# A hybrid mLSTM and attention layer on one core: the turn of v, the norm's small operations and the sums of two products are placed and shared out differently

## The chip, the cores and the metric

The kernel runs on one core of a Trainium2 chip. The core has a matmul engine (PE, with a separate loader for its weights, PEld), and DVE, ACT and POOL for elementwise work; each works through its own queue in order. SP only issues transfers; POOL issues some too. The metric is the device time of one execution in microseconds (us), lower is better. The kernel before takes 1559.74 us, the median of three runs (1558.71 to 1560.47).

## The reference

One layer over 512 prompt frames and 64 frames of a running stream, with width 1024, in fp32:

```python
h = layer_norm(ALPHA * x + 0.5 * swiglu_ffn(x, ffn1_w_gu, ffn1_w_down), ln1_g, ln1_b)
mix, new_state = token_mixer(h, ...)
h = layer_norm(ALPHA * h + mix, ln2_g, ln2_b)
h = layer_norm(ALPHA * h + 0.5 * swiglu_ffn(h, ffn2_w_gu, ffn2_w_down), ln3_g, ln3_b)
```

The mixer multiplies h with one wide matrix, w_in, and splits the columns into the mLSTM's q, k, v, o, i, f, the attention's q, k, v, and two gates. The mLSTM has 4 heads of 256: a causal convolution of width 4 and a silu on q and k, then a chunked recurrence with exponential gates. The attention has 16 heads of 64 over a band of 8 chunks of 64 frames, with a bias by relative position; the running stream has 256 past keys and values. The two branches are projected, gated, added and multiplied with w_out. Besides the frames the new states are returned, the rows of k and v among them. layer_norm subtracts the mean, multiplies by rsqrt(variance + 1e-5), then by g, and adds b.

## The kernel before

All 576 frames stay in SBUF, features on the partitions: a tile (a "slot", tag s) is 128 features x 576 frames, worked on in two halves (hf) of columns. An fp32 factor is split into a high part (wh, hi), rounded to the matmul's input type, and a low part (wl, lo), the rest; a product is three matmuls: wh·hi, wh·lo, wl·hi. Large products are done in units of seven block products instead of eight (Strassen's way), for which sums of inputs are formed first: class Combos. Its method add makes four sums from two input tiles, make splits the sums in two parts.

**How a low part is made.** Either DVE subtracts the high part from the source, or add_lo (L195) does it: ACT copies the high part with a factor -1, and a transfer issued by POOL adds the source to it in flight. Weights pass through pump: SP loads a raw tile wr (two buffers), ACT makes wh, and DVE or add_lo makes wl (four buffers). Weights of w_in are named ("in", column); those in ADDED (L179) take add_lo, those in PIECES (L177) are converted in halves of 512 columns.

**What sets the order.** Python writes the program. The order on PE is written by hand: a model clock counts each matmul (122 for 288 columns), and later(dt, fn) places a piece dt units behind the present point. ACT, DVE, POOL and SP get their orders from a list scheduler; hot(n) and high_priority(offset=n) raise an operation in it, and tc.issue_after(x) forces an order. On the chip each queue is in order.

**The norm** (class Norm, L498 on; three times). stats (L633) sums on PE, takes the variance and rs = variance to the power -0.5 (on POOL), and builds dg, the identity scaled by rs, on DVE; centre (L699) subtracts the mean from the eight tiles of the half, the tiles in CP (L185 to L188) on POOL and the others on DVE; spread multiplies dg with ones on PE, so that each partition has every frame's rs, L_SPREAD or L_SPREAD1 (first FFN's norm) units behind stats; apply does the rest. The last half of the last norm is turned (L671): frames go to the partitions by transposes into four PSUM tiles of 512 columns, (block b, half of the features q). DVE subtracts the mean and multiplies by g from PSUM, then multiplies by rs and adds b, and SP stores: eight large DVE operations behind PE's last matmul.

**The first FFN** splits its sums with make (own parts all through add_lo). **The projection** (os_split, L1757 on) makes its sums with add, one turn of a loop for each of four pairs of tiles.

**The attention** runs over j, eight pairs of heads. att_qkv(j) (L1408) computes a pair's q, k, v; within it v_tr (L1442) transposes v so that frames lie on the partitions (tile vc; ACT evicts the high part, DVE the low), placed 8000 units behind its start for j of 2 and more, and v_past (L1431) splits the past values on POOL, at 9500. att_core(j) (L1515) follows: scores, the transposes of the probabilities, and the products with v. There ttr (L1541) adds the bias to a score tile and takes the row minimum (mx) in one DVE operation, at hot(20).

**The mLSTM head** h: the convolution (conv_rest, L1862) ends in a silu on ACT (qf, then qk), and weights (L2003), five blocks b placed 11000 + 2600 b units behind the head's start, multiplies q with k.

In the profile, L135 is the line of the helper that records every matmul, L145 that of transposes, L149 of ACT, L152, L155 and L159 of elementwise operations, L196 of add_lo's transfers; the tile's name tells which step it is.

Of the kernel before, what the change touches and what calls it, by code (L numbers as in the profile page):

```python
# [10 lines left out]
F32 = mybir.dt.float32  # L11
# [6 lines left out]
P = 128  # L18
# [70 lines left out]
def tile_layer(ctx: ExitStack, tc: tile.TileContext, ins, outs):  # L89
# [75 lines left out]
    def blank(out, like, behind=None):  # L165
# [10 lines left out]
    NH0, NH1 = 1, 6  # L176
    PIECES = {("in", 48), ("in", 40), ("in", 32)}  # L177

    ADDED = {("in", c + j) for c in (32, 40, 48) for j in range(2, KT)} | {("in", c) for c in (*range(2, 8), *range(10, 32), *range(56, 72))} \  # L179
        | {("gu2", 1, 1), ("gu2", 2, 0), ("gu2", 2, 1)}  # L180
# [4 lines left out]
    EARLY1 = [("in", 16), ("in", 17)]  # L185
    CP = (6, 7)
    GR = 2150
    L_MEAN, L_STATS, L_SPREAD, L_SPREAD1 = 300, 1440, 4920, 3600  # L188
    plan = []
# [308 lines left out]
    class Norm:  # L498
# [134 lines left out]
        def stats(self, hf):  # L633
            lp = self.lp
            s1, s2 = self.hs(self.s1, hf), self.hs(self.s2, hf)
            n = self.H[hf][1]
            nb = len(blocks_(n))
            st, bc = bank(), bank()[:, :n]
            self.sums(hf, st, 0, (s1,))
            mm(bc, ones_d, s1, True, True)  # L640
            self.sums(hf, st, 1, (s2,))
            with tc.high_priority(offset=HOT):
                rs, power = self.rsqrt(hf, st)

                dg = lp.tile([P, 320], F32, tag="sq", name=nm("dg"), bufs=2)[:, :n]
                tt(dg[:, 0:2 * P].rearrange("p (b c) -> p b c", c=P), ident.unsqueeze(1).to_broadcast([P, 2, P]),
                   rs[:, 0:2].unsqueeze(2).to_broadcast([P, 2, P]), ALU.mult)
                if nb == 3:
                    ts(dg[:, 2 * P:], ident[:, 3 * P - n:], rs[:, 2:3], None, ALU.mult)
            later(L_MEAN, lambda: self.centre(hf, bc, power))  # L650
            later(self.spread_at, lambda: self.spread(hf, dg))
# [16 lines left out]
        def turned(self, hf, dh, sq):  # L668
# [16 lines left out]
            with tc.high_priority(offset=HOT):  # L685
                m = self.lp.tile([P, 3], F32, tag="m2", name=nm("m"), bufs=2)
                act(m[:, :nb], st[:, 0:nb])
                rs, _ = self.rsqrt(hf, st)
            z = {}
            for q in range(2):  # L690
                for b in range(nb):
                    z[b, q] = slot(F32)[:, :512]
                    last = stt(z[b, q], pts[b, q], m[:, b:b + 1], self.gb[q], ALU.subtract, ALU.mult)
            with tc.issue_after(last.ins):
                for (b, q), t in z.items():
                    stt(t, t, rs[:, b:b + 1], self.gb[2 + q], ALU.mult, ALU.add)
                    SP.dma_start(outs["yt"][b, :, q * 512:(q + 1) * 512], t)

# [55 lines left out]
    class Combos:  # L754


        def __init__(self, xs, raw, sums, nx=NX):
            self.xs, self.raw, self.n, self.sums, self.nx = xs, raw, 0, sums, nx
            self.b = {}

# [3 lines left out]

        def add(self, i):
            r1, r2 = self.raw[4 + i], self.raw[i]
            a, b = slice(0, HT_), slice(HT_, T)
            u, v = self.sums[2 * i], self.sums[2 * i + 1]
            tt(u[:, a], r1[:, a], r1[:, b], ALU.subtract)
            stt(v[:, a], u[:, a], -1.0, r2[:, b], ALU.mult, ALU.subtract)  # L770
            tt(u[:, b], r2[:, b], r1[:, b], ALU.subtract)
            return stt(v[:, b], v[:, a], -1.0, r2[:, a], ALU.mult, ALU.subtract)

        @hot(80)
        def make(self, middle):
# [3 lines left out]
            for n, (ka, kb) in ((1, ("t2", "t4")), (0, ("t1", "t3"))):  # L779
                for i in range(4):  # L780

                    t, hi, lo = self.sums[2 * i + n], self.tile(), self.tile()
                    with tc.issue_after(after.ins) if after is not None else nullcontext():
                        last = ACT.activation(hi, t, AF.Copy)
                        self.added = add_lo(lo, hi, t)
                    d = self.b.setdefault(i, {})
                    d[ka], d[kb] = (hi[:, a], lo[:, a]), (hi[:, b], lo[:, b])
# [341 lines left out]
    def ffn(xs, n, gi, raw, final=None, prev=None):  # L1129
        hh = {}  # L1130
        with tc.tile_pool(name=nm("hr"), bufs=FT, side="right", reuse_waits="tile") as hr, \
# [20 lines left out]

            combos = Combos(xs, raw, [hr.tile([P, T], F32, tag="h", name=nm("h"), bufs=FT + 1) for _ in range(8)])
            j0 = CL[n]
            un = GateUp(n, j0, hr, None, None, combos)
# [251 lines left out]
    def att_qkv(j):  # L1407
# [30 lines left out]

        later(11500 if j < 2 else 9500, v_past)
        vf = vf0 if j == 0 else slot(F32)  # L1440
# [18 lines left out]
        elif j:  # L1459
            SP.dma_start(vf, AV[j])  # L1460
            SP.dma_start(outs["v"][:, j, :], vf)
        later((12500, 2240, 8000)[min(j, 2)], v_tr)

# [59 lines left out]
    def att_core(j, st):  # L1523
# [16 lines left out]

        @hot(20)  # L1541
        def ttr(out, ps, g, acc):
# [67 lines left out]
        def values_s(th, tl):  # L1610
# [6 lines left out]
            for e in range(2):  # L1617
                act(o_[64 * e:64 * e + 64, NP_:T], po[0:64, 64 * e:64 * e + 64])

        t = 4500 if j else 7000  # L1620
        for e in range(2):
# [115 lines left out]
    for j in range(6):  # L1737
# [3 lines left out]
        if j == 3:  # L1741
# [20 lines left out]
            def os_split():  # L1762
# [24 lines left out]
                for i in range(4):  # L1787
                    combos.sums[2 * i] = slot(F32)
                    combos.add(i)
                    halves(i, 1)  # L1790
# [73 lines left out]
    def conv_rest(R, ct, scale, room, tail=None):  # L1864
# [5 lines left out]
        hi, lo = room(), room()  # L1870
        with tc.issue_after(order["exp"].ins) if "exp" in order else nullcontext():
            for a, b, u in ((0, NP_, 0), (NP_, T, NP_ + 3)):
# [112 lines left out]
    def ml_early(h, st):  # L1985
# [34 lines left out]
        for b in range(5):  # L2020
            later(11000 + 2600 * b, lambda b=b: weights(b))

# [255 lines left out]
```

## Time and profile before

| | us |
|---|---|
| median of three runs | 1559.74 (1558.71 to 1560.47) |
| the profiled execution, as timed | 1559.26 |
| its span in the trace | 1557.5 |
| PE busy | 1533.1 |
| DVE busy | 1140.8 |
| ACT busy | 890.3 |
| POOL busy | 223.8 |

The profile is of one execution. The span runs from the first to the last recorded instruction; the 1.76 us beside it lie around the program. A row of a group of instructions gives line, engine, operation, output <- input with shape, then the count, the busy time and the mean of one; a number in square brackets is the engine's idle time just before an instruction, with what ended it.

### The profile page before, as it was taken

The numbers are of one execution on the slowest core, as the hardware profiler recorded it, in microseconds if no ns is written. First come the engines' busy times: TensorE is split into PE (matmuls) and PEld (weight loads), VectorE is DVE, ScalarE is ACT, GpSimd is POOL, SyncE is SP. The second block draws the span as 40 slices with busy tenths as digits, with TensorE's granted clock in tenths as the row PEclk, the third lists the DMA queues.
The fourth block names the chain that finished last, engine by engine and source line by source line (L and its number), as shares of the span: only waits on it lengthen the run. The fifth ranks groups of instructions, "written<-read, shape, count | busy, mean of one in ns | idle before, by whom it ended". The sixth has DMA issues, their size and how long they took to land.

```text
span 1557.5 us, 29496 instructions
## 1 busy us (share of the span) xinstructions
PE 1533.1 (98%) x11579; PEld 1516.2 (97%) x11579; DVE 1140.8 (73%) x2118; ACT 890.3 (57%) x1670; POOL 223.8 (14%) x433
## 2 busy tenths in 40 slices
PE   9999999999999999999999999999999999999998
PEld 9999999999899999999999999999999999999997
DVE  7777778676998766676596666755776877788766
ACT  7545447433866467777754877753456454557333
POOL 2000000000210025554301222202111000001000
PEclk9999999999999999999999999999999999999999
DMA  9322223533764448676534764652655222225434
GB/s 269 114 95 96 92 98 91 141 105 118 192 171 144 141 143 209 177 188 162 128 134 139 176 157 113 166 159 86 197 146 134 105 86 103 88 70 132 133 112 149
DMA packets 80836, 212.66 MB, mean 137 GB/s; under 512 B 9145, under 2 KB 21049, under 8 KB 80697
## 3 DMA queue, kind: packets, MB, share of 16 engines
q1 hardware_dynamic: 65432, 170.07, 33.1%
q0 software_dynamic: 12096, 34.87, 12.9%
q10 hardware_dynamic: 3168, 5.83, 1.1%
q8 instruction: 91, 1.49, 0.4%
q14 instruction: 49, 0.39, 0.1%
HBM read 173.18 MB, written 21.63 MB: 125 GB/s over the span
## 4 chain that ended last, share of the span: by engine, by line
PE 80%; DVE 6%; ACT 6%; DMA 3%; issue 2%; POOL 2%; SPq 0%; DVEq 0%; ACTq 0%; POOLq 0%
PE mm L135 65%; PE aux L135 14%; PE aux L145 2%; ACT s L149 1%; DVE wl L152 1%; DMA wr<-in_w_gu 1%; DVE s L152 1%; ACT sc L149 1%; ACT wh L149 1%; POOL kh L159 1%; DMA kl<-kl 1%; DVE s L155 1%; DVE U L155 0%; DMA wr<-in_w_dn 0%; DMA c<-in_C 0%
## 5 line engine op out<-in xcount | busy, mean ns | idle before, releaser
L135 PE MATMUL mm<-s,wh 128*128 128x288 f32 (+2 forms) x3667 | 752.9, 298 | 4.7 <-DVE s L152 2.1
L135 PEld LDWEIGHTS mm<-s,wh 128*128 128x128 f32 x3667 | 587.3, 189 | 9.7 <-DVE s L152 2.9
L135 PE MATMUL mm<-s,wl 128*128 128x288 f32 (+2 forms) x1806 | 533.2, 295 | 0.0
L135 PEld LDWEIGHTS mm<-s,wl 128*128 128x128 f32 x1806 | 340.0, 188 | 0.2 <-DVE wl L152 0.2
L149 ACT ACTIVATE wh<-wr 128x1024 fp32r<-128x1024 f32 (+2 forms) x135 | 134.4, 1003 | 167.0 <-PE mm L135 102.1
L152 DVE TENSOR_TENSOR wl<-wr,wh 128x1024 fp32r<-128x1024 f32 (+2 forms) x95 | 110.0, 1167 | 51.5 <-ACT wh L149 51.1
L135 PE MATMUL mm<-tx,wh 128*128 128x288 f32 x677 | 140.5, 296 | 1.1 <-DVE tx L152 1.0
L135 PEld LDWEIGHTS mm<-tx,wh 128*128 128x128 f32 x677 | 109.2, 188 | 1.6 <-DVE tx L152 1.2
L152 DVE TENSOR_TENSOR wl<-wt,wh 128x1024 fp32r<-128x1024 f32 x51 | 63.7, 1248 | 56.9 <-ACT wh L845 56.9
L135 PE MATMUL mm<-tx,wl 128*128 128x288 f32 x350 | 103.2, 295 | 0.0
L845 ACT ACTIVATE wh<-wt 128x1024 fp32r<-128x1024 f32 x51 | 54.0, 1059 | 85.3 <-DVE wt L152 85.3
L152 DVE TENSOR_TENSOR wl<-wu,wh 128x1024 fp32r<-128x1024 f32 x63 | 77.1, 1224 | 29.4 <-ACT wh L845 29.3
L845 ACT ACTIVATE wh<-wu 128x1024 fp32r<-128x1024 f32 x63 | 66.7, 1058 | 39.9 <-PE mm L135 34.1
L135 PE MATMUL mm<-tx,ah 128*128 128x288 f32 x416 | 85.5, 297 | 0.0
L196 POOL DMA_DIRECT2D s<-s x16 | 13.7, 854 | 466.7 <-DVE hb L152 424.0
L149 ACT ACTIVATE h<-h 128x288 f32<-128x288 f32 x78 | 34.0, 436 | 59.9 <-DVE h L152 59.8
L135 PEld LDWEIGHTS mm<-tx,ah 128*128 128x128 f32 x416 | 66.2, 188 | 0.7 <-ACT c L149 0.4
L135 PEld LDWEIGHTS mm<-tx,wl 128*128 128x128 f32 x350 | 65.7, 188 | 0.0
L152 DVE TENSOR_TENSOR wl<-ws,wh 128x1024 fp32r<-128x1024 f32 x51 | 62.2, 1220 | 4.2 <-ACT wh L845 4.2
L152 DVE TENSOR_TENSOR ws<-wu 128x1024 f32<-128x1024 f32 (+1 forms) x55 | 64.7, 1177 | 0.0
L135 PE MATMUL mm<-h,wh 128*128 128x288 f32 (+2 forms) x304 | 62.7, 296 | 0.1
L135 PE MATMUL mm<-tx,al 128*128 128x288 f32 x208 | 61.1, 294 | 0.0
(395 smaller groups left out, 3466.7 us busy)
## 6 DMA issues: line engine op xcount, KB each, us to landing
wu<-in_w_gu SPq DMA_DIRECT2D x78, 512.0 KB, 4.3
wr<-in_w_in SPq DMA_DIRECT2D x48, 512.0 KB, 3.8
wr<-in_w_dn SPq DMA_DIRECT2D x38, 512.0 KB, 3.6
wl<-in_w_in POOLq DMA_DIRECT2D x36, 512.0 KB, 6.2
wu<-in_w_in SPq DMA_DIRECT2D x24, 512.0 KB, 4.9
wr<-in_w_dn SPq DMA_DIRECT2D x20, 384.0 KB, 3.5
s<-s POOLq DMA_DIRECT2D x16, 288.0 KB, 4.7
wu<-in_w_ap SPq DMA_DIRECT2D x8, 512.0 KB, 4.7
```

Of the source, the lines that this page charges most:

```text
L135: PE.matmul(out, lhsT, rhs, start=start, stop=stop, **kw)
L145: PE.transpose(out, in_, idn)
L149: return ACT.activation(out, in_, func, **kw)
L152: return (eng or DVE).tensor_tensor(out, a, b, op=op)
L155: return DVE.scalar_tensor_tensor(out=out, in0=a, scalar=s, in1=b, op0=op0, op1=op1)
L159: return (eng or DVE).tensor_scalar(out=out, in0=a, scalar1=s1, scalar2=s2, op0=op0, **kw)
L196: return POOL.dma_start(lo, src, accum_op=ALU.add)
L845: self.last = ACT.activation(hi, src, AF.Copy)
```

## The change

Seven edits, none of which changes what PE multiplies:

- the weights ("in", 48) and ("in", 40), the first of attention's w_in columns, go from PIECES to ADDED: they are converted whole, and their low part comes from add_lo
- CP is (4, 5, 6, 7) for (6, 7): POOL subtracts the mean from four of eight tiles. L_SPREAD1 is 3200 for 3600
- dg is made by ACT, one copy of the identity with a scale for each block of 128 frames
- in turned one of the four tiles, own = (nb-1, 0), leaves DVE: a small DVE operation makes -mean·rs, ACT applies scale and bias from PSUM, POOL multiplies by g and adds b
- Combos gets begin, which makes two of the four half sums of a pair on POOL, and own: with own = 2 the first FFN's make lets DVE subtract two low parts that add_lo made. The projection begins the next pair's sums a loop turn ahead, which takes one slot more
- for j of 2 and more v_tr and v_past go from att_qkv(j) to att_core(j), 800 and 2500 units behind its start; ttr is at hot(120)
- the silu is raised by 60, and the blocks of weights of head 0 are placed 1800 units later

```diff
-    PIECES = {("in", 48), ("in", 40), ("in", 32)}
+    PIECES = {("in", 32)}
-    ADDED = {("in", c + j) ...
+    ADDED = {("in", 48), ("in", 40)} | {("in", c + j) ...
-    CP = (6, 7)
+    CP = (4, 5, 6, 7)
-    L_MEAN, L_STATS, L_SPREAD, L_SPREAD1 = 300, 1440, 4920, 3600
+    L_MEAN, L_STATS, L_SPREAD, L_SPREAD1 = 300, 1440, 4920, 3200
...
-                tt(dg[:, 0:2 * P].rearrange("p (b c) -> p b c", c=P), ident.unsqueeze(1).to_broadcast([P, 2, P]),
-                   rs[:, 0:2].unsqueeze(2).to_broadcast([P, 2, P]), ALU.mult)
-                if nb == 3:
-                    ts(dg[:, 2 * P:], ident[:, 3 * P - n:], rs[:, 2:3], None, ALU.mult)
+                for b, t0 in enumerate(blocks_(n)):
+                    c0 = b * P
+                    act(dg[:, c0:min(c0 + P, n)], ident[:, max(c0 + P - n, 0):], scale=rs[:, b:b + 1])
...
+            own = nb - 1, 0
             for q in range(2):
                 for b in range(nb):
                     z[b, q] = slot(F32)[:, :512]
-                    last = stt(z[b, q], pts[b, q], m[:, b:b + 1], self.gb[q], ALU.subtract, ALU.mult)
+                    if (b, q) != own:
+                        last = stt(z[b, q], pts[b, q], m[:, b:b + 1], self.gb[q], ALU.subtract, ALU.mult)
+                    else:
+                        with tc.issue_after(last.ins):
+                            last = stt(m[:, nb:nb + 1], m[:, b:b + 1], -1.0, rs[:, b:b + 1], ALU.mult, ALU.mult)
+                        t = z[own]
+                        act(t, pts[own], AF.Identity, scale=rs[:, b:b + 1], bias=m[:, nb:nb + 1])
+                        tt(t, t, self.gb[0], ALU.mult, POOL)
+                        tt(t, t, self.gb[2], ALU.add, POOL)
+                        SP.dma_start(outs["yt"][b, :, 0:512], t)
             with tc.issue_after(last.ins):
                 for (b, q), t in z.items():
-                    stt(t, t, rs[:, b:b + 1], self.gb[2 + q], ALU.mult, ALU.add)
-                    SP.dma_start(outs["yt"][b, :, q * 512:(q + 1) * 512], t)
+                    if (b, q) != own:
+                        stt(t, t, rs[:, b:b + 1], self.gb[2 + q], ALU.mult, ALU.add)
+                        SP.dma_start(outs["yt"][b, :, q * 512:(q + 1) * 512], t)
...
+            self.own = 4
...
+        def begin(self, i):
+            r1, r2 = self.raw[4 + i], self.raw[i]
+            a, b = slice(0, HT_), slice(HT_, T)
+            u = self.sums[2 * i]
+            tt(u[:, a], r1[:, a], r1[:, b], ALU.subtract, POOL)
+            tt(u[:, b], r2[:, b], r1[:, b], ALU.subtract, POOL)
+
-        def add(self, i):
+        def add(self, i, begun=False):
...
-                        self.added = add_lo(lo, hi, t)
+                        if n or i < self.own:
+                            self.added = add_lo(lo, hi, t)
+                        else:
+                            tt(lo, t, f(hi), ALU.subtract)
...
+            if prev is None:
+                combos.own = 2
...
-        later(11500 if j < 2 else 9500, v_past)
+        if j < 2:
+            later(11500, v_past)
...
-        later((12500, 2240, 8000)[min(j, 2)], v_tr)
+        if j < 2:
+            later((12500, 2240)[j], v_tr)
+        else:
+            st["turn"] = v_tr, v_past
...
-        @hot(20)
+        @hot(120)
         def ttr(out, ps, g, acc):
...
+        for dt, fn in zip((800, 2500), st.get("turn", ())):
+            later(dt, fn)
...
-                    combos.sums[2 * i] = slot(F32)
-                    combos.add(i)
+                    if i == 0:
+                        combos.sums[0] = slot(F32)
+                    if i < 3:
+                        combos.sums[2 * i + 2] = slot(F32)
+                        combos.begin(i + 1)
+                    combos.add(i, i > 0)
...
-        with tc.issue_after(order["exp"].ins) if "exp" in order else nullcontext():
+        with tc.high_priority(offset=60), tc.issue_after(order["exp"].ins) if "exp" in order else nullcontext():
...
-            later(11000 + 2600 * b, lambda b=b: weights(b))
+            later((11000 if h else 12800) + 2600 * b, lambda b=b: weights(b))
```

More of the change, by code (lines that the diff above doesn't have):

```diff
@@ L176, in tile_layer @@
     NH0, NH1 = 1, 6
-    PIECES = {("in", 48), ("in", 40), ("in", 32)}
-    ADDED = {("in", c + j) for c in (32, 40, 48) for j in range(2, KT)} | {("in", c) for c in (*range(2, 8), *range(10, 32), *range(56, 72))} \
+    PIECES = {("in", 32)}
+    ADDED = {("in", 48), ("in", 40)} | {("in", c + j) for c in (32, 40, 48) for j in range(2, KT)} | {("in", c) for c in (*range(2, 8), *range(10, 32), *range(56, 72))} \
         | {("gu2", 1, 1), ("gu2", 2, 0), ("gu2", 2, 1)}
@@ L768, in add @@
             u, v = self.sums[2 * i], self.sums[2 * i + 1]
-            tt(u[:, a], r1[:, a], r1[:, b], ALU.subtract)
+            if not begun:
+                tt(u[:, a], r1[:, a], r1[:, b], ALU.subtract)
             stt(v[:, a], u[:, a], -1.0, r2[:, b], ALU.mult, ALU.subtract)
-            tt(u[:, b], r2[:, b], r1[:, b], ALU.subtract)
+            if not begun:
+                tt(u[:, b], r2[:, b], r1[:, b], ALU.subtract)
             return stt(v[:, b], v[:, a], -1.0, r2[:, a], ALU.mult, ALU.subtract)
```

## The prediction

> **What bounds the kernel now.** I read the page first, then the waits of the matmul engine, then its windows by stage.
>
> ```profile
> span 1557.5 us, 29496 instructions
> PE 1533.1 (98%) x11579; PEld 1516.2 (97%) x11579; DVE 1140.8 (73%) x2118; ACT 890.3 (57%) x1670; POOL 223.8 (14%) x433
> PE 80%; DVE 6%; ACT 6%; DMA 3%; issue 2%; POOL 2%; SPq 0%; DVEq 0%; ACTq 0%; POOLq 0%
> ```
>
> PE, the matmul engine, is busy for 1533.1 of 1557.5 us, and the chain that ends last runs over it for 80%. The change keeps every matmul, so it can only win from the 24.4 us in which PE stands still. Who ends those idle times (total us, times, longest):
>
> ```profile
> PE aux L145 <- POOL sc L159: 2.5, 4, 0.8
> PE aux L145 <- DVE vc L152: 2.3, 3, 0.8
> PE mm L135 <- DVE s L152: 2.1, 5, 0.9
> ...
> PE aux L135 <- DVE qk L155: 1.1, 1, 1.1
> PE mm L135 <- DVE tx L152: 1.0, 1, 1.0
> PE aux L145 <- DVE mx L1543: 0.8, 3, 0.3
> PE aux L135 <- DVE wl L152: 0.7, 1, 0.7
> ...
> PE mm L135 <- DMA s<-h: 0.7, 1, 0.7
> PE aux L135 <- ACT qk L149: 0.6, 1, 0.6
> PE mm L135 <- ACT s L149: 0.6, 1, 0.6
> ```
>
> And by stretch: from:to, length, busy time of PE, PEld, DVE, ACT, POOL, then the granted clock:
>
> ```profile
> 34.00:44.00 10.00, 8.62 (x62) 7.97 (x61) 8.04 (x10) 6.10 (x11) 1.72 (x2) 1.00 0.95 225
> 395.00:415.00 20.00, 17.51 (x125) 15.69 (x124) 18.29 (x44) 15.90 (x39) 6.38 (x10) 1.00 0.72 222
> 580.00:777.00 197.00, 190.62 (x1507) 184.80 (x1507) 130.77 (x420) 147.07 (x353) 100.65 (x194) 1.00 0.69 176
> 797.00:807.00 10.00, 8.87 (x65) 8.42 (x64) 9.93 (x18) 5.28 (x11) 0.00 (x0) 1.00 0.36 113
> 880.00:890.00 10.00, 8.34 (x58) 7.46 (x57) 6.86 (x13) 6.87 (x16) 2.70 (x9) 1.00 1.03 241
> 1140.00:1171.00 31.00, 30.92 (x232) 30.07 (x231) 25.56 (x61) 19.50 (x43) 6.92 (x8) 1.00 0.51 134
> 1549.00:1557.50 8.50, 0.94 (x9) 0.70 (x7) 5.04 (x8) 0.00 (x0) 0.37 (x1) 0.81 0.33 123
> ```
>
> PE's idle time, length less busy, is thus 1.38 us in the first units, 2.49 behind the first norm, 6.38 in the attention, 1.13 in the projection, 1.66 at the first mLSTM head and 0.08 at the second norm; in the last stretch, 7.56, only the tail is left. At 1.00 the clock has nothing to give in the stages. What the change can reach at most is these sums.
>
> **First units** (sums' low parts, own = 2). Two waits make up the 1.38: 0.65 us for a transfer and 0.7 for DVE's weight part.
>
> ```profile
> 42.02 0.40 PE L135 MATMUL mm<-s,wh 128*128 128x288 f32 x1 [0.65 <-DMA s<-h]
> s<-s POOLq DMA_DIRECT2D x16, 288.0 KB, 4.7
> L152 DVE TENSOR_TENSOR s<-s,c 128x288 f32<-128x288 f32 x12 | 5.0, 445 | 0.0
> ```
>
> The awaited transfer is one of those that add a low part (4.7 us each); two of them go, and with each an ACT copy. DVE gets two subtractions of 576 columns, by the third row (288 columns in 445 ns) 4 x 0.45 = 1.8 us, and in this window it is free for 10.00 - 8.04 = 1.96. They fit, just. I take 0.65 and a third of the other wait: **+0.9**. Ends: both waits go, +1.4; or DVE's 1.8 all stands before the weight part that PE awaits, 0.65 - 1.8 = -1.1.
>
> **First norm and w_in.** Three edits meet: POOL takes four of eight subtractions, ACT makes the diagonal, and the weights 48 and 40 get their low part from a transfer, with the spread matmul 400 model units (a 288-column matmul counts 122 and takes 1533.1/11579 = 0.13 us, so 0.4 us) earlier.
>
> ```profile
> L152 POOL TENSOR_TENSOR s<-s,c 128x288 f32<-128x288 f32 x4 | 3.5, 892 | 0.0
> L152 DVE TENSOR_TENSOR dg<-ident,rs 128x256 f32<-128x256 f32 x2 | 2.1, 1028 | 1.1 <-POOL rs L495 1.1
> L149 ACT ACTIVATE kwh<-aux,tcol 128x128 fp32r<-128x128 f32 x32 | 11.7, 366 | 6.2 <-DVE kwl L155 5.0 <-PE aux L145 1.2
> DMA to landing us min/median/max: 5.2/6.2/10.1
> 386.94 1.15 ACT L149 ACTIVATE wh<-wr 128x512 fp32r<-128x512 f32 x2 [1.45 <-PE mm L135]
> 389.35 0.63 ACT L149 ACTIVATE wh<-wr 128x512 fp32r<-128x512 f32 x1 [1.25 <-PE mm L135]
> 389.23 0.65 PE L135 MATMUL aux<-dg,one 128*128 128x288 f32 x2
> 396.06 0.38 PE L135 MATMUL mm<-s,wh 128*128 128x256 f32 x1 [0.59 <-ACT s L149]
> ```
>
> Per half DVE loses two subtractions, 0.9 us, and the diagonal's 1.03 for its two large blocks; the four weight halves go too. POOL pays 4 x 0.89 = 3.6 for its subtractions, ACT three copies at 0.37, 1.1 us (0.7 without the short third). DVE is 18.29 of 20 us busy in this window, so what PE awaits there (0.6 from ACT, 2.1 from DVE) should come on time: 2.49. Against it stands weight 40. Its buffer comes free at 389.35; two ACT passes over 1024 columns (four halves of 0.63 less overlap, some 2.1 us) bring the issue of its transfer to 391.5, or with the diagonal in between to 392.2. It lands 6.2 us later, at 397.7 or 398.4, by the row for the transfers of this kind (all of them issued in later stages, so this is an estimate). PE, which runs a fixed order, reaches the first of these products at 396.06 - 0.59 = 395.5 and needs weight 40 some four matmuls later, at 396.0: a stall of 1.7 or 2.4 that takes the place of the old ones. I take the first, since nothing makes the diagonal go ahead: 2.5 - 1.7 = **+0.8**. Ends: no stall, +2.5; a landing in 10.1 us, at 402.3, a stall of 6.3, -3.8.
>
> The Trainium skill ("DMA: Bandwidth & Descriptors", section on the anatomy of one DMA) prices a POOL-queue transfer at 2.0 us plus bytes/436e3, an estimate of 3.2 us for 512 KB; by it weight 40 would land at 394.7 to 395.4 without a stall, and this term would be 2.5. The trace disagrees: its minimum is 5.2.
>
> **Attention** (turn of v a stretch later, score minima hotter). Every second pair shows the same three waits, 0.81, 0.25 and 0.56, three times.
>
> ```profile
> 664.30 0.88 DVE L152 TENSOR_TENSOR vc<-aux,vc 128x512 fp32r<-128x512 f32 x2 [0.32 <-ACT vc L149]
> 666.73 4.64 DMA kl<-kl
> 671.47 0.40 POOL L159 TENSOR_SCALAR kh<-kp 64x256 fp32r<-64x256 f32 x1
> 677.22 0.66 PE L145 MATMUL aux<-ident,sc 128*128 128x128 f32 x4 [0.56 <-POOL sc L159]
> ```
>
> The turn's 0.88 us on DVE, behind which PE waits, goes to the following stretch, and with it what the past values' split puts on POOL; the three waits are the only ones of each pair, so there is room in the other stretch. The first wait goes, and the second with it, as DVE's 128x320 minima rise in the queue: 2.3 + 0.8 = 3.1. The third is POOL's: its chain of ten operations up to the scores begins when the copy of kl lands (666.73 + 4.64 = 671.37). DVE makes kl behind vc, so the copy can start up to 0.88 earlier while PE comes 0.81 + 0.25 earlier; that wait grows by 0.2, three times 0.6. **+2.5**. Ends: all three go, 3 x 1.62 = +4.9; the turn finds the same wait at its new place, and POOL doesn't move at all, 3.1 - 2.4 - 3 x 0.6 = -1.1.
>
> **Projection** (sums begun on POOL). The window's row shows DVE 9.93 of 10 us busy and POOL not at all. Six subtractions leave DVE, 6 x 0.45 = 2.7 us, and cost an idle POOL 6 x 0.89 = 5.3, a loop turn ahead of their use. The 1.0 us that PE waits for DVE's tx goes: **+1.1**, the window's whole idle time. Other end: the begin waits for the extra slot and each of three sums comes 2 x 0.45 later: at most -0.9 x 3 + 1.1 = -1.6.
>
> **First head** (silu raised, weights 1800 units later).
>
> ```profile
> 880.37 1.05 ACT L149 ACTIVATE wh<-wr 128x1024 fp32r<-128x1024 f32 x1
> 882.22 0.79 ACT L149 ACTIVATE qf<-U 128x512 f32<-128x512 f32 x2
> ```
>
> PE's two waits are for qk, made from the silu (qf), which stands behind a 1.05-us conversion. Raised past it, which puts that conversion 0.8 later, and with the scores 1800/122 x 0.13 = 1.9 us later, 2.9 us cover waits of 0.6 + 1.1. **+1.7**, or 1.1 if the move alone does little. Below that only if PE's fill is itself late, which the window (no other wait) doesn't show.
>
> **Second norm:** 0.08 idle, **+0.1**; the diagonal coming late there is a rival below.
>
> **Tail.** Behind PE's last matmul stand eight 512-column DVE operations.
>
> ```profile
> 1551.31 2.73 DVE L155 SCALAR_TENSOR_TENSOR s<-s,rs,s 128x512 f32<-128x512 f32 x4
> L152 POOL TENSOR_TENSOR gm<-gm,s 128x320 f32<-128x320 f32 x4 | 3.5, 873 | 11.1 <-DVE s L152 11.1
> L152 POOL TENSOR_TENSOR gm<-gm,s 128x256 f32<-128x256 f32 x4 | 3.0, 739 | 7.8 <-issue 5.9 <-DVE s L152 1.9
> ```
>
> Two of them go (2 x 0.68), a small one of some 0.2 comes: DVE ends 1.2 earlier, at 1554.04 - 1.2 = 1552.9. POOL's slope is 134 ns for 64 columns, so 512 cost 873 + 192 x 2.1 = 1.28 us. Eight of 0.68 started at about 1554.04 - 5.5 = 1548.5; behind the first and the small one, an ACT copy (0.7, by 0.63 for 512 columns) starts at 1549.4, and POOL's two end at 1552.7, with DVE. **+1.0**; The upper end is DVE's 1.2. The lower: by the other row (892 ns for 288 columns) POOL takes 1.6 each and ends at 1553.3, and with its transfer ahead of the other three in SP's queue they all wait for that: 0.7, or 0.1 if ACT's copy waits as long again.
>
> The Trainium skill ("GPSIMD Engine Reference", section on performance versus the Vector engine) has POOL at some 2.6 cycles an element where DVE needs one, which speaks against giving POOL two of eight operations here. With it 512 columns would be an estimate of 2.6 x 0.53 = 1.4 us beside a fixed part, POOL would end last and the term would be about 0.7. The rows' 892 against 445 ns are a ratio of 2.0.
>
> **Sum.** 0.9 + 0.8 + 2.5 + 1.1 + 1.7 + 0.1 + 1.0 = 8.1. New orders on ACT, DVE and POOL will open a wait or two of the size of those listed (0.6, 0.7); I charge one, leaving 7.5. The profiled execution took 1559.26 us (1557.5 and 1.76 around it); the median of three runs is 1559.74, so the forecast is 1559.74 - 7.5 = **1552.2**.
>
> **Rivals.** *POOL takes the attention's wait over* (18%): the copy of kl lands no earlier, so the third wait grows by all of the 1.06 that PE gains, three times, 3.2 in all where I took 0.6: 1554.8. For it: the 4.64-us copy stands on the chain; against: DVE makes kl behind vc.
>
> *A late transfer* (12%): weight 40 lands after 10.1 us; the norm's term is -3.8 for 0.8: 1556.8. For it: that maximum, and a DMA share of 0.72 in this stage; against: the median of 6.2.
>
> *An early one* (4%): weight 40 lands within 4 us, and the norm's term is 2.5 for 0.8: 1550.5. Against: the minimum of 5.2. The skill's fit on that page leads here; the trace so far doesn't bear it out.
>
> *Each wait has a second one close behind it* (12%), from an input as late as the first (ACT's s beside DVE's, a buffer not free). Then only head and tail are left, 1.7 + 1.0, less new waits of as much: 1559.7. For it: DVE is 73% busy over the span, so it is mostly an order and not a load that makes PE wait.
>
> *Slower* (9%): the diagonal on ACT. ACT works in order, and conversions of weights stand in it at each norm. At 386.94 two halves end at 388.1; if the second passes of 48 and 40 and the first of 40 (1.05 each) then come ahead of the diagonal (1.1), it is done at 392.4. PE's spread matmul was at 389.23 and is now due 0.4 earlier, 388.8: a stall of 3.6 in each of two halves of two norms, 14.4, against 7.5: 1566.6. It decides from (7.5 + 3.1)/4 = 2.7 us a half. Against it: in 1140 to 1171 ACT is busy for 19.50 of 31 us, so its queue is seldom three deep.
>
> **Chances.** Forecast 45%, the rivals 18, 12, 4, 12 and 9. A measurement of this kernel can tell 0.2%, 3.1 us, from no change. Faster: 45 + 18 + 12 + 4 = 0.79; same 0.12; slower 0.09. The range leaves out above the slower rival and the upper part of the one before it, 1559.0. Below, it holds the early transfer together with attention's upper end, 1552.2 - 1.7 - 2.4 = 1548.1, so 1548.0.
>
> **What would show it.** In the changed kernel's waits of PE the rows for DVE vc, DVE tx, DVE qk, DMA s<-h and DVE mx should be gone; DVE s should shrink below 1; POOL sc should stay near 2.5 to 3.1; and a new wait for a transfer into wl of 1.7 to 2.4 us should stand at 396. PE's idle time should be 0.5 in 34:44, 2 in 395:415 and near 0 in 797:807 and 880:890, and the tail about 1 us shorter. Wrong would be: a wait of PE on dg, a wl that lands after 400, or POOL sc above 5.

## The result: 1562.22 us, slower by 0.16%

The changed kernel takes 1562.22 us (median of 20 runs, 1560.93 to 1564.74) against 1559.96 us (20 runs of the kernel before beside them): a ratio of 1.0016, 95% interval 1.0009 to 1.0023. The forecast was 1552.2, in a range from 1548.0 to 1559.0.

The page of the changed kernel's profile, then its waits of PE (total us, times, longest):

```profile
span 1559.9 us, 29496 instructions
PE 1535.5 (98%) x11579; PEld 1520.6 (97%) x11579; DVE 1140.2 (73%) x2090; ACT 893.8 (57%) x1683; POOL 246.9 (16%) x451
```

```profile
PE mm L135 <- DMA wl<-in_w_in: 5.6, 2, 3.3
PE mm L135 <- DVE s L152: 1.6, 3, 0.8
...
PE mm L135 <- DVE st L155: 0.9, 1, 0.9
PE aux L145 <- POOL sc L159: 0.9, 3, 0.4
PE mm L135 <- DVE tx L152: 0.8, 1, 0.8
PE aux L145 <- DVE ptl L152: 0.8, 1, 0.8
PE aux L145 <- DVE vl L152: 0.8, 1, 0.8
PE aux L145 <- DVE mx L1572: 0.7, 1, 0.7
```

The waits that the change was aimed at are gone: DVE vc, DVE qk, ACT qk, DVE wl, the transfer into s. In their place stands one of 5.6 us, in two pieces, for the low parts of two weights. The windows by stage, with the columns of before (PE, PEld, DVE, ACT, POOL, granted clock):

```profile
34.00:44.00 10.00, 10.00 (x76) 9.76 (x75) 8.78 (x12) 5.90 (x11) 0.00 (x0) 1.00 0.58 156
395.00:415.00 20.00, 15.44 (x90) 14.83 (x91) 11.35 (x22) 8.26 (x21) 5.61 (x8) 0.74 0.59 201
580.00:777.00 197.00, 193.54 (x1529) 187.99 (x1528) 138.00 (x425) 150.90 (x361) 104.97 (x202) 1.00 0.71 179
797.00:807.00 10.00, 9.20 (x68) 8.97 (x68) 9.20 (x14) 4.38 (x8) 2.82 (x3) 1.00 0.23 74
880.00:890.00 10.00, 10.00 (x74) 9.75 (x73) 7.14 (x13) 7.50 (x17) 3.16 (x9) 1.00 1.01 235
1140.00:1171.00 31.00, 30.06 (x225) 29.18 (x224) 23.64 (x52) 19.97 (x47) 11.05 (x12) 1.00 0.56 137
```

The second row tells the story: PE idle for 4.56 us, and a mean clock of 0.74, where before had 1.00. So PE's busy time grew too, 1535.5 us for 1533.1 with the same 11579 matmuls.

PE issues the same number of matmuls in both kernels, so the start of the n-th one in both traces gives the shift between them, stage by stage (us; minus is a gain):

| stage (matmul numbers) | shift at its end | change within | forecast |
|---|---|---|---|
| first units (to 300) | -1.71 | -1.7 | -0.9 |
| first norm and w_in (to 4200) | +4.54 | +6.2 | -0.8 |
| attention (to 5400) | +1.21 | -3.3 | -2.5 |
| projection (to 6300) | +1.52 | +0.3 | -1.1 |
| first head (to 7200) | +0.42 | -1.1 | -1.7 |
| second norm (8400 to 9300) | +0.78 | +0.9 | -0.1 |
| other stretches (to 11578) | +0.90 | -0.5 | +0.6 |
| tail, from there to the span's end: 9.34 for 7.80 | +2.44 | +1.5 | -1.0 |

The table compares two single executions. How far such a shift can be trusted shows in the first units: three_back and cp_none, two kernels of the experiments below, run the same instructions in the same order on every engine for the first 45 us, and their shifts there are -1.28 and +0.09.

Four terms of the forecast have the wrong sign: the first norm with w_in, the projection, the second norm and the tail. The experiments below take them up. Some of them ran on different chips, each beside the kernel before, so they are compared by their ratio to it.

### The profile page after: what moved, and what is told of

Its sections match the earlier page's. It is cut to its first block, busy times and chain, and to the rows that moved or that the text cites. A ratio compares the mean times of both kernels' runs of the same rounds, so it can differ in the third digit from the quotient of the medians.

```text
span 1559.9 us, 29496 instructions
## 1 busy us (share of the span) xinstructions
PE 1535.5 (98%) x11579; PEld 1520.6 (97%) x11579; DVE 1140.2 (73%) x2090; ACT 893.8 (57%) x1683; POOL 246.9 (16%) x451
## 4 chain that ended last, share of the span: by engine, by line
PE 83%; DVE 6%; ACT 5%; DMA 2%; issue 2%; POOL 2%; DVEq 0%; SPq 0%; POOLq 0%; ACTq 0%
PE mm L135 67%; PE aux L135 14%; PE aux L145 2%; DVE wl L152 1%; DVE s L152 1%; ACT s L149 1%; ACT wh L149 1%; DMA wl<-in_w_in 1%; DMA w<-in_w_gu 1%; ACT sc L149 1%; POOL kh L159 0%; DMA wr<-in_w_dn 0%; DVE s L155 0%; ACT wh L868 0%; DVE sc L1572 0%
## 5 line engine op out<-in xcount | busy, mean ns | idle before, releaser
L196 POOL DMA_DIRECT2D s<-s x16 | 13.7, 859 | 469.5 <-DVE hb L152 217.7
```

The lines of the kernel that those rows point to most:

```text
L196: return POOL.dma_start(lo, src, accum_op=ALU.add)
```

## Experiments

### The two late transfers

**Edits.** pieces_back undoes one line in the changed kernel, only_added makes the same edit alone in the kernel before:

```diff
-    PIECES = {("in", 32)}
-    ADDED = {("in", 48), ("in", 40)} | {("in", c + j) ...
+    PIECES = {("in", 48), ("in", 40), ("in", 32)}
+    ADDED = {("in", c + j) ...
```

> The changed kernel, with weights 48 and 40 converted in halves on ACT and DVE again (their low part no longer from a transfer). Theory: the two late transfers cost the waits of 5.6 us and, by the matmuls at half clock up to 408.6, another 4 to 5 us. Then the time falls by 9 to 10 us less what the old waits for DVE in 395 to 415 (2.5 us) bring back: 8 us, to about 1554, ratio to before 0.996, with the clock at 1.00 in 395 to 415. Rival: what costs is DVE slowed by POOL's subtractions, twice as many as before; then the waits for DVE take the place of the waits for the transfers, and the time falls by less than 3 us.

> The kernel before with one edit of the change alone: the low parts of weights 48 and 40 from transfers. Theory: the loss is that edit's by itself, 5 to 8 us: about 1566, with waits for wl and a clock of 0.50 behind them. Rival: the transfers land late only because the rest of the change moved them among the loads for the next units (issued at 390.6 to 392.7); in the kernel before the loads are issued from 392.3 on and the transfers land in 5 to 6 us, with a loss under 2 us.

**Measured.** pieces_back 1554.97 us, ratio 0.9970 (0.9959 to 0.9982); only_added 1563.65 us, 1.0028 (1.0017 to 1.0039). With this one edit undone the changed kernel is faster than before. By itself the edit costs 4.4 us, less than the 5 to 8 expected, and PE waits for its two low parts as long as in the changed kernel (2.36 and 3.17 us for 2.25 and 3.35); in the company of the others it costs 7.2 us; what makes the difference isn't shown. The late landing is thus the edit's own. The gain of pieces_back is 7 us, where 8 were expected, since waits for DVE come back (3.0 us in all, on a clock of 1.00):

```profile
PE mm L135 <- DVE s L152: 3.0, 5, 1.4
395.00:415.00 20.00, 17.80 (x127) 16.45 (x127) 18.23 (x43) 16.12 (x41) 6.48 (x9) 1.00 0.58 181
```

The theory held. The rival's price, a gain under 3 us, did not come; what it says of POOL's subtractions is taken up below.

### Why they are late

In the changed kernel the trace's DMA view of 385 to 406 us has these rows (a queue's packets, MB and share of the engines' time; then an issue's count, size and median us to landing):

```profile
q1 hardware_dynamic: 1288, 4.39, 55.2%
q0 software_dynamic: 288, 1.05, 28.9%
...
wl<-in_w_in POOLq DMA_DIRECT2D x2, 512.0 KB, 8.7
```

The two transfers (issued at 388.33 and 390.68) are all of q0. Per MB they hold the engines for 28.9/1.05 = 27.5 units where plain loads hold them for 55.2/4.39 = 12.6, 2.2 times the engine time. No run separates what the adding does from what the queue does. Four loads of 512 KB for the next units stand beside them, and four loads of other weights. Three runs were to hold the loads for the next units back; in the first two (loads_later, loads_later2) the requested order didn't hold, or held for one load of four, and the landing stayed at 9.5 us for weight 40. Their times, 1562.34 and 1562.29 us, are the changed kernel's again and tell nothing of the loads. The third made it a dependence of the data:

```diff
-    un.load(0)
-    un.load(1)
...
     wst["ahead"] = 2
+    un.load(0, qf0)
+    un.load(1, qf0)
...
+                if gate is not None:
+                    act(w[:, 1024 * e:1024 * e + 1], gate[:, 0:1])
                 SP.dma_start(w[:, 1024 * e:1024 * e + 1024], self.srcs[j][e])
```

> The changed kernel with the four loads of 512 KB for the next units issued only behind the transfer of weight 40's low part. If these loads make the accumulating transfers late, both land 5 to 6 us after their issue instead of 7.8 and 9.5, the waits for wl fall from 5.6 to about 2 us and the clock holds: about 1556, unless the loads are then late themselves. If an accumulating transfer takes that long by itself, the waits stay at 5 us or more.

> As loads_later, whose loads went out at 390.9 to 394.0 all the same, so that it told nothing; now they are issued behind ACT's eviction of the first half of q, after the two transfers have landed. If the loads make the transfers late: landing 5 to 6 us after the issue, waits for wl of 1 to 2.5 us instead of 5.6, clock at 1.00, and 3 to 7 us less time, as far as the loads' own landing (some 10 us later than before) is not awaited then. If the transfers take 7.8 and 9.5 us by themselves: waits as in the changed kernel.

> The changed kernel with the four loads of 512 KB held back by a data dependence: one column of each buffer is written by ACT from the first half of q, so a load can't go out before about 403 (in loads_later and loads_later2 the order asked for didn't hold the loads). If the loads make the accumulating transfers late: landing 5 to 6 us after the issue, waits for wl of 1 to 2.5 us for 5.6, clock at 1.00 in 397 to 405, and up to 5 us less time if the loads aren't awaited later. If the transfers take 7.8 and 9.5 us by themselves: waits of 5 us or more again.

**Measured** in loads_gated, first the same DMA view's row, then two of PE's waits:

```profile
wl<-in_w_in POOLq DMA_DIRECT2D x2, 512.0 KB, 7.6
```

```profile
PE mm L135 <- DMA wl<-in_w_in: 4.0, 2, 2.2
PE mm L135 <- DVE st L155: 3.3, 1, 3.3
```

Without the four loads the transfers land after 7.4 and 7.8 us (7.8 and 9.5 with them). So the four loads make up 1.6 us of PE's wait. The rest, 4.0 us, stays with the transfers overlapping each other and with the few loads left in this stage; no run parts these two, and which of them it is stays open. The result lies between the two cases of the expectation. The loads are then awaited later (3.3 us for st), and the whole is slower, 1565.75 us, 1.0040 (1.0025 to 1.0055). The gain expected from 5 to 6 us of landing was not to be had: two of these transfers that overlap don't land in that time here.

### What the clock adds

The changed kernel's PE at the two waits, and its windows around them:

```profile
396.21 0.39 PE L135 MATMUL mm<-s,wl 128*128 128x256 f32 x1 [2.25 <-DMA wl<-in_w_in]
396.44 0.41 PE L135 MATMUL mm<-s,wh 128*128 128x256 f32 x2
400.19 0.58 PE L135 MATMUL mm<-s,wl 128*128 128x256 f32 x1 [3.35 <-DMA wl<-in_w_in]
```

```profile
395.00:397.00 2.00, 0.63 (x3) 0.42 (x3) 2.00 (x5) 1.57 (x4) 0.99 (x3) 1.00 1.05 279
397.00:399.00 2.00, 0.00 (x0) 0.00 (x0) 0.77 (x3) 0.04 (x1) 0.00 (x0) 0.92 1.08 281
399.00:401.00 2.00, 0.81 (x4) 0.81 (x5) 0.00 (x0) 0.00 (x0) 0.00 (x0) 0.50 1.00 379
...
407.00:409.00 2.00, 2.00 (x12) 2.00 (x11) 2.00 (x4) 1.85 (x6) 2.00 (x3) 0.52 0.00 0
409.00:411.00 2.00, 2.00 (x18) 2.00 (x18) 2.00 (x3) 1.48 (x3) 2.00 (x3) 1.00 0.00 0
```

The clock falls to 0.50 at 398.7, while PE waits, and stays there until 408.9, though PE is busy again from 400.2: 12 matmuls fit into 2 us there, and 18 from 409 on. fill_gaps2 puts work without use into the two gaps (fill_gaps had it in the like product at the second norm as well):

```diff
+                            if tiles[0][0][0] == ("in", 48) and p == 0 and k == 0 and hf == hl[0] and t < 2:
+                                if t == 0:
+                                    dummy = bank()
+                                for _ in range((17, 25)[t]):
+                                    PE.matmul(dummy[:, :HALVES[hf][1]], wh[:, ww], hs(xh, hf), start=True, stop=True)
                             if wl is not None:
```

> The changed kernel with 17 and 25 extra matmuls of 256 columns (2.0 and 2.9 us, results unused) in front of the two matmuls that wait for the low parts of 48 and 40, so that the matmul engine stays busy while it waits. If the fall of the clock to 0.50 is a cost of its own that comes from the idle time, the clock stays at 1.00 and the time falls by the 4 to 5 us that the matmuls from 400 to 408.6 lose, to about 1558, although the transfers land no earlier. If the idle time alone counts, and the clock fell for another reason, the time stays at 1562.

> The changed kernel with 17 and 25 unused matmuls of 256 columns ahead of the two waiting matmuls at the first norm alone (fill_gaps had them at the second norm too, which cost 4.9 us there). Theory: the clock stays at 1.00, the transfers land as late as before, and the matmuls between 400 and 409 win 3 to 4 us: about 1559. If the transfers alone counted: 1562.

**Measured** in fill_gaps2, two windows and two waits of PE:

```profile
397.00:401.00 4.00, 3.85 (x33) 3.65 (x32) 2.31 (x5) 2.42 (x6) 0.00 (x0) 1.00 1.01 332
401.00:405.00 4.00, 4.00 (x35) 3.90 (x34) 0.00 (x0) 0.00 (x0) 0.00 (x0) 1.00 0.90 368
```

```profile
PE mm L135 <- DVE st L155: 1.8, 1, 1.8
PE aux L135 <- ACT dg L149: 1.5, 1, 1.5
```

The clock stays at 1.00 although the transfers land at 396.4 and 400.1 as before. So the fall comes from the idle time, as the theory has it, and at this place it is worth 4.0 us: the changed kernel's matmul 2960 starts at 405.31 instead of 409.31. But the time is 1562.21 us, 1.0016 (1.0007 to 1.0025), the changed kernel's. ACT and DVE had been held up by the same transfers; PE now meets them, in waits of 1.5 us for dg and 1.8 for st (0.9 in the changed kernel; the new one halves the clock as well, for 3.4 us), and by the attention its lead is 0.6 us. The forecast of 1559 was a miss: a faster PE in a stretch is no gain while what it feeds on comes late. fill_gaps, 1565.14 us, 1.0038 (1.0024 to 1.0051), carries 4.9 us of extra matmuls at the second norm, and is otherwise the same.

The length of a wait alone doesn't decide whether the clock falls. In loads_gated the one of 3.3 us left it at 1.00 (454 to 459). In the kernel before, waits of 0.59, 0.38 and 0.89 us (395.5 to 399.1) left it at 1.00; in att_proj, whose order of work is the same up to there, waits of 0.54, 0.38 and 0.89 us brought it down behind them:

```profile
399.00:401.20 2.20, 2.09 (x16) 1.00 0.90 339
401.30:404.60 3.30, 3.30 (x17) 0.50 0.88 343
404.70:407.00 2.30, 2.30 (x22) 1.00 0.10 41
```

(The columns are PE's busy time, the clock, the share of the DMA engines and GB/s.) What is common to all the traces is the length of the stretches at 0.50 between the first and the last 20 us: 3.4, 6.8, 10.2 or 13.7 us, one to four times 3.41. This fits a clock that is set anew every 3.41 us, by what PE did in the stretch that has just ended, so that the same wait counts in full or is split between two stretches. In loads_gated such a border at 456.3, counted on in steps of 3.41 us from the clock's last change at 408.5, splits the wait of 3.3 us into 1.7 and 1.6. That is a reading of the traces, not an experiment.

The Trainium skill ("TensorE: Matmul & The Clock Gate", Part 1) has the clock halved after an idle window of some 3.4 us and raised after one busy window. The traces agree on the length of the window, but it need not be idle throughout: in the 3.41 us ahead of the fall PE was busy for 0.6 us in the changed kernel and for 2.5 in att_proj. That the clock took three windows to come back in the changed kernel (398.7 to 408.9) goes with a wait in the first and mostly single-column sums (402.5 to 405.9) in the second.

### POOL beside DVE: the tail

tail_back has the eight DVE operations of before in turned. tail_one_input keeps the change's tail, but POOL's two operations read one tensor each and leave out g and b for that quarter of the last half:

```diff
-                        tt(t, t, self.gb[0], ALU.mult, POOL)
-                        tt(t, t, self.gb[2], ALU.add, POOL)
+                        ts(t, t, 1.5, 0.25, ALU.mult, ALU.add, eng=POOL)
+                        ts(t, t, 1.5, 0.25, ALU.mult, ALU.add, eng=POOL)
```

> The changed kernel with the eight large DVE operations of the tail as before. Theory: POOL's two operations of 512 columns (2.93 us) held DVE's three beside them (1.46, 1.75 and 0.74 us where 0.68 was usual), and its store went ahead of the other three, so the stretch behind the last matmul grew by 1.5 us; with the old tail that comes back: 1560.7. Rival: the sharing gains the 1.0 us of the prediction and the longer end comes from the stores: then the time rises by 0 to 1 us.

> The changed kernel with POOL's two operations of the tail on one input each (a constant scale and offset; g and b are left out for that quarter of the last half). If DVE is slowed because both engines read two inputs from SBUF, DVE's three operations beside them go back from 1.46 and 1.75 us to some 0.7, and the stretch behind the last matmul shrinks from 9.3 to 8 us: about 1560.8. If any POOL operation slows DVE, they stay at 1.4 to 1.7 while POOL works.

**Measured.** The timeline of the changed kernel's tail, then that of tail_one_input:

```profile
1551.41 2.93 POOL L152 TENSOR_TENSOR s<-s,s 128x512 f32<-128x512 f32 x2 [1.14 <-ACT s L149]
1551.76 3.79 DVE L155 SCALAR_TENSOR_TENSOR s<-s,rs,s 128x512 f32<-128x512 f32 x3
1554.37 0.33 SPq L702 DMA_DIRECT2D out_yt<-s  x1
1554.79 1.38 SPq L707 DMA_DIRECT2D out_yt<-s  x3
```

```profile
1551.85 1.63 POOL L159 TENSOR_SCALAR s<-s 128x512 f32<-128x512 f32 x2 [1.16 <-ACT s L149]
1552.19 2.49 DVE L155 SCALAR_TENSOR_TENSOR s<-s,rs,s 128x512 f32<-128x512 f32 x3
```

Three DVE operations take 3.79 us, where before had four in 2.73: one by one 1.46 and 1.75 us beside POOL, and 0.74 when POOL is done. Beside one-input operations two take 0.82 and 1.09, and the third, behind them, 0.74. DVE thus ends at 1555.55 (1554.04 before). Of the four stores POOL's goes out first, at 1554.37, and the last at 1555.76, where before they had been spread from 1552.08 to 1554.07. tail_back is at 1560.86 us, 1.0009 (1.0000 to 1.0019), and the stretch behind the last matmul at 7.80 us again; tail_one_input has 1561.26 us, 1.0014 (1.0005 to 1.0024), and 8.06 us. Both times are near what was expected, but their intervals overlap the changed kernel's, so the loss is read from the stretch behind the last matmul and not from the times. By it the sharing is a loss, and most of the slowing, not all, needs two inputs on POOL.

The Trainium skill ("GPSIMD Engine Reference", Specifications) states DVE's half of this: POOL shares its SBUF interfaces with VectorE, with contention where a DVE instruction has two SBUF inputs. The rows agree: 1.46 and 1.75 us against 0.74.

### POOL beside DVE: the norms

The rows of the mean's subtraction on DVE, first in the changed kernel at the first norm (the kernel before, where POOL took two of eight, has 445 ns, as the prediction shows), then at the second norm in the kernel before and in the changed one:

```profile
L152 DVE TENSOR_TENSOR s<-s,c 128x288 f32<-128x288 f32 x8 | 5.1, 683 | 0.0
```

```profile
L152 DVE TENSOR_TENSOR s<-s,c 128x320 f32<-128x320 f32 x6 | 2.6, 480 | 0.0
L152 DVE TENSOR_TENSOR s<-s,c 128x320 f32<-128x320 f32 x4 | 3.2, 824 | 0.0
```

At the first norm eight take 5.1 us now, twelve took 5.0: DVE has won nothing by giving four away, and POOL spends 3.6 us more. two_back undoes the weights' edit and the tail, three_back also CP; cp_none leaves POOL no subtraction, CP = (). In three_back:

```diff
-    CP = (4, 5, 6, 7)
+    CP = (6, 7)
```

> The changed kernel with weights 48 and 40 in halves again and the old tail; POOL still takes four of eight subtractions in every norm. If the two costs add up: 1555.0 less the 1.4 us of the tail, 1553.5, ratio to before 0.996. If the tail's end is set by something else, 1555.

> As two_back, and POOL takes two of the eight subtractions again. Theory: beside POOL's operations DVE's subtractions took 683 ns instead of 445 at the first norm and 824 instead of 480 at the second, so four on POOL make both engines late: the waits for DVE's s (3.0 us at 395 to 415, 0.9 at 1160 to 1165) shrink by 2 to 3 us and the time falls to about 1551. Rival: DVE needs the relief, and the waits grow: 1555 or more.

> As three_back, with all eight subtractions of the mean on DVE. Theory: POOL's operations slow DVE's beside them by as much as they take off; then none on POOL is worth about as much as two: 1550 to 1552.5, DVE's subtractions at 0.42 to 0.45 us each. Rival: two on POOL are the right number, and DVE's two more make PE wait 1 to 2 us longer: 1553 to 1555.

**Measured.** On one chip two_back 1554.48 us, 0.9968 (0.9957 to 0.9980), and three_back 1551.07 us, 0.9947 (0.9934 to 0.9960): 3.4 us for CP alone. By the starts of the matmuls 2.2 of them lie at the first norm and 1.0 at the second. two_back itself is a miss: it was to be 1.4 us faster than pieces_back (0.9970), and the ratios are the same within their intervals. Its tail is 1.4 us shorter in the trace (7.81 for 9.20), but its first units came 1.1 us later and its clock was at 0.50 for 3.4 us from 399.3 on. cp_none, on another chip, has 0.9966 (0.9953 to 0.9978), 1553.40 us. Where the time goes shows at the second norm, in DVE's work beside and behind POOL's subtractions, first in two_back, then in three_back:

```profile
1155.67 1.10 DVE L152 TENSOR_TENSOR s<-s,s 128x256 fp32r<-128x256 f32 x1
1157.77 1.08 DVE L152 TENSOR_TENSOR s<-s,s 128x256 fp32r<-128x256 f32 x1
```

```profile
1153.61 1.10 DVE L152 TENSOR_TENSOR s<-s,s 128x256 fp32r<-128x256 f32 x1
1155.04 0.41 DVE L152 TENSOR_TENSOR s<-s,s 128x256 fp32r<-128x256 f32 x1
```

DVE's other two-input operations are slowed as well, the splits of the other half here, for as long as POOL works: 4.3 us for four subtractions, 2.3 for two. So four subtractions and three splits take DVE 5.4 us in two_back (from 1154.17), and six and three take it 4.9 in three_back (from 1152.11). In three_back PE is busy for 18.47 of the 20 us, DVE for 19.12:

```profile
395.00:415.00 20.00, 18.47 (x140) 17.86 (x139) 19.12 (x48) 18.19 (x44) 6.12 (x8) 1.00 0.66 195
1140.00:1171.00 31.00, 30.82 (x227) 30.19 (x226) 28.22 (x68) 20.87 (x48) 5.67 (x7) 1.00 0.54 145
```

So three_back's theory holds: four on POOL is a loss against two. Whether two are better than none isn't shown. cp_none's time is in the range of its rival, but the intervals of the two ratios overlap, and 1.4 us of its lag stand in the first 45 us, where both kernels run the same order of instructions.

**The diagonal** is the norm's third edit. four_back is three_back with dg on DVE:

> As three_back, and the norm's diagonal is made by DVE again: what is left of the change is the first units, the projection, the attention, the first head and the earlier spread. If the diagonal on ACT was a gain (DVE loses 1.9 us a half), the waits for DVE's s in 395 to 415 rise from 0.6 to 2 us and the time from 1551.1 to 1552 to 1553. If it was none, because ACT evicts the later (ACT vf, 1.5 us at 405 in three_back), the time is 1550 to 1551.

**Measured** 1556.63 us, 0.9985 (0.9975 to 0.9994), 0.38% over three_back (from the two ratios), more than expected. Its windows:

```profile
395.00:415.00 20.00, 17.17 (x118) 16.36 (x119) 18.26 (x44) 16.03 (x39) 5.73 (x9) 0.91 0.70 218
401.00:405.00 4.00, 4.00 (x22) 4.00 (x23) 3.23 (x7) 2.02 (x6) 2.57 (x3) 0.57 0.25 100
```

PE waits 2.5 us for DVE's s, and here too the clock falls behind the waits (0.57 in 401 to 405, 22 matmuls in 4 us against 34 in three_back). The diagonal on ACT is the edit of the norm that pays, in the company of the earlier spread: four_back keeps L_SPREAD1 at 3200, which wants the diagonal sooner, and at this norm it is 2.7 us behind the kernel before, which has the diagonal on DVE too. No run undoes the spread by itself.

### The attention alone

att_only makes the attention's edits in the kernel before, att_proj those and the projection's (begin on POOL):

> The kernel before with the attention's edits alone (turn of v and split of the past values later, score minima at 120). The prediction had 2.5 us for them, and the matmuls of the changed kernel came 3.3 us nearer between 573 and 732 us. Theory: they are a gain by themselves, 2.5 to 3.5 us: about 1556, with the waits for vc gone. Rival: the gain in the changed kernel came from its other order, and alone they give under 1 us.

> The kernel before with the attention's and the projection's edits. att_only gained 3.4 us up to 731 us and lost 5.2 between 766 and 811, with a wait of 2.1 us for ACT's tx and the clock at 0.75. Theory: the matmul engine, 4.5 us early, meets DVE and ACT busy with the projection's sums, and the two subtractions a turn that POOL takes over make the room: the loss falls below 1 us and the time is about 1556. Rival: the loss has another cause, and the time stays at 1560 to 1561.

**Measured.** att_only 1561.02 us, 1.0017 (1.0007 to 1.0028); att_proj 1556.47 us, 0.9984 (0.9974 to 0.9993). The window of the projection in both:

```profile
797.00:807.00 10.00, 7.03 (x37) 6.58 (x36) 7.53 (x14) 3.77 (x6) 0.00 (x0) 0.75 0.45 159
```

```profile
797.00:807.00 10.00, 9.21 (x68) 8.76 (x67) 8.73 (x14) 5.17 (x11) 0.00 (x0) 1.00 0.46 166
```

Within the attention att_only wins 3.3 us, as much as the changed kernel. It loses them from 799 on: PE, 4.5 us early (1.0 of them from the first units, which this kernel doesn't change), waits 2.1 us for ACT's tx and 0.9 for DVE's behind DVE's chain of sums, and then runs at half clock up to 808.8. A second fall at the first head (887.3 to 890.7) costs another 1.4. With the sums shared out, the wait for ACT is gone, the clock holds and the gain stays. att_proj comes to the projection only 2.8 us early, but that is not the reason: three_back, which shares the sums too, comes 6.4 us early and loses 0.4 there. Without the projection's edit the attention's is thus worth nothing. The projection's edit alone was not run; in the changed kernel its own stage lost 0.3.

## Why the prediction was wrong

**First norm and w_in, forecast +0.8, measured -6.2: the step that failed.** The mechanism was named, a stall for weight 40's low part at 396; its size was not, and what it does to the clock was left out. First, the landing was taken as 6.2 us, the middle of transfers from other stages; weight 40's took 9.5 us. That is 3.3 of the 3.9 us by which PE's wait of 5.6 us exceeds the 1.7 of the forecast. Four loads beside it make up 1.6 us (loads_gated); what keeps the rest is open. Weight 48, which the prediction left out, stalled PE first, for 2.25 us, but these lie within the delay that 40's landing sets. That PE came there 1.7 us sooner made no difference: the transfer for 48 went out some 5.6 us before PE came for it in the changed kernel as in tail_back, tail_one_input and loads_gated, however early PE was, and in only_added, where PE came 2.4 us later, the waits were 2.36 and 3.17 us.

Second, "at 1.00 the clock has nothing to give" put the clock at nothing. The stall halved it for 10.2 us, worth 4.0 us on PE (fill_gaps2). The 3.9 and the 4.0 us make up more than the 7.0 us by which the term is off. The sentence was right for the profiled execution of the kernel before (mean clock 0.999), not for the kernel: of its 31 executions beside loads_later2, 20 have a lower mean clock, down to 0.994. The rival of a late transfer had the mechanism, but at 4.6 us over the forecast it was priced without the clock. The prediction's own sign of being wrong, a wl that lands after 400, came true (400.15).

**POOL's share, forecast as relief for DVE.** The sum subtracted 0.9 us a half from DVE and let POOL work beside it at 0.89 us each. The runs show that POOL's work slows DVE's beside it: 683 ns for 445 in the first norm, 824 for 480 in the second, 1.46 and 1.75 us for 0.74 in the tail. That cost 0.9 us at the second norm (forecast 0.1 gained), 1.5 in the tail (forecast 1.0 gained) and 2.2 at the first norm (two_back against three_back). The prediction weighed POOL's speed there, not the sharing. POOL's own price was near: 1.26 and 1.59 us for 1.28 each. (The 1.4 us that it set beside this multiplies a time by a ratio of cycles of two engines, which is not a ratio of times; its own rows give 2.0.)

**The other terms.** First units +1.7 for +0.9: both waits went, but part of the 1.7 is luck. The 13 traces with this edit reach matmul 300 at 45.5 us in the mean (44.5 to 46.8), the four without it at 46.6 (45.7 to 47.3), so the edit is worth some 1.2, and no run undoes it alone. Attention +3.3 for +2.5: the wait for vc went, as forecast; that for the minima stayed at two places (mx, 0.7 and 0.3 for 0.8), and POOL's shrank instead of growing (sc, 0.9 for 2.5); the rival by which POOL takes the wait over did not come true. Projection -0.3 for +1.1: the wait for tx shrank only from 1.0 to 0.8; what the edit is worth shows in att_proj. First head +1.1 for +1.7: its own waits went, a new one of 0.8 us (DVE vl) came 24 us later. The slower rival, a diagonal behind conversions on ACT, is refuted: ACT's three copies went first, and PE waited for dg nowhere in the changed kernel.

**The version without the three edits.** three_back keeps the diagonal on ACT, the attention, projection, first units, head and the earlier spread, and is faster than both kernels: 0.9947 (0.9934 to 0.9960). Of these, first units, projection, head and spread were never tried alone.

## What to carry to other kernels

A stall of PE can halve its clock and cost far more than its length: 5.6 us of waits brought 4.0 us more here. A term that may stall PE must be priced with the clock, as a chance: 3.3 us of waiting left it alone in loads_gated, and less than 2 us in three pieces halved it in att_proj but not in the kernel before. So one profile at a clock of 1.00 doesn't say that a kernel is free of it. Giving POOL two-input work while DVE reads two inputs from SBUF moved no load here, since DVE lost as much beside it; give POOL what can run while DVE is idle, or give the work to ACT, as the diagonal was. A gain at one stage brings PE early to the next, so the edit that makes room there has to come with it (att_only against att_proj).

## What the hardware showed beyond that

- The stretches at half clock lasted 3.4, 6.8, 10.2 or 13.7 us: 10.2 in the changed kernel (398.7 to 408.9), 6.8 in att_only (802.0 to 808.8), 3.4 in att_proj, two_back and four_back, 13.7 in only_added.
- Of the 31 executions of the kernel before beside loads_later2, the 11 with a mean clock of 0.999 took 1557.28 to 1558.55 us, the nine with 0.996 and less 1559.93 to 1561.78.
- A transfer that adds to its target in flight held the DMA engines 2.2 times as long per MB as a plain load in the changed kernel (27.5 against 12.6 units) and 1.9 times in loads_gated (27.0 against 13.9), and two together took 7.3 to 9.6 us each for 512 KB in all runs that had them.
- One-input operations on POOL also slow DVE a little: 0.82 and 1.09 us for 0.74.
